# A two-layer hybrid trunk on one core: raw tokens into the first products, constants on another queue, a later rotation table and a shorter tail

## The chip, the cores and the metric

One core of one Trainium2 chip runs the whole program. The metric is the device time of one execution in microseconds (us). The engines are TensorE (PE in the profile; its weight loads are PEld), VectorE (DVE), ScalarE (ACT), GpSimd (POOL) and SyncE (SP). SP does no arithmetic: it issues DMAs, as ACT and POOL can too ("SPq", "ACTq", "POOLq").

## What is computed

The input x has 256 tokens of 1024 float32 values. Each of two layers normalises the stream, makes one large input projection, runs three token mixers side by side, projects and merges them, and adds the result to the stream:

```
for layer in range(2):
    h = rms_norm(x, norm_w[layer])                 # x * rsqrt(mean(x*x) + 1e-6) * norm_w
    proj = einsum('bsd,de->bse', h, w_in[layer])
    (a_xbc, a_z, a_dt, b_q, b_k, b_v, b_z,
     c_q, c_k, c_v, c_f, c_z, gates) = split(proj, split_at, axis=-1)
    y_a = mamba2_branch(a_xbc, a_z, a_dt, conv_w, conv_b, dt_bias, a_log, d_skip, ssm_norm_w)
    y_b = sliding_window_branch(b_q, b_k, b_v, b_z, sinks, cos, sin)
    y_c = forgetting_attention_branch(c_q, c_k, c_v, c_f, c_z, f_bias)
    branch = einsum('bsiw,iwd->bsid', stack([y_a, y_b, y_c]), w_proj[layer])
    merged = sum(sigmoid(gates + gate_bias) * branch)
    x = x + einsum('bsd,de->bse', merged, w_out[layer])
return rms_norm(x, final_norm_w)
```

The sliding-window branch rotates its queries and keys with a table of cosines and sines (`rope`). The document calls the projections by their letters: K, V and Q are `b_k`, `b_v`, `b_q`; CV is `c_v`; dt/f are the 16 columns of `a_dt` and the 16 of `c_f`.

## The kernel before

**Products.** Every product with a weight matrix is made in three passes of a reduced float32 format: each operand is split into a high part (`hi`, a copy on ACT, L259) and the rest (`lo`, a subtraction on DVE, L260; at the start half of them on POOL, L1149), and hi·hi, lo·hi and hi·lo are added up in one PSUM bank (`dense`, L273). Products of tokens in rows have the tokens' hi and lo as the stationary side; 256 tokens are two halves t of 128 rows. There are three PSUM banks for products (`mm`) and five for all else (`mx`).

**The stream of weights.** All weights come through one list, in the order in which the program uses them, as pieces of 512 KB. `load_to` (L327) issues them on SP's queue into six buffers named `raw`; `feed` (L358) splits a piece once fewer than four split pieces are held, and a new load is issued when a split has freed its buffer. The dt/f weights are a small load of their own in the same list (two DMAs, 64 KB), with their own split at L259 and L260. The hardware queues have eight lanes: a DMA waits for the landing of the one issued eight earlier.

**Order of the work.** PE's order is that of the program. Beside the list of products (from L1044) the program keeps a set of generators (attention, scan, transposes), which `launch` (L102) puts in with a due time, and `pump` and `drain` (L129, L139) take from between products by a clock of PE's work. The order on DVE, ACT and POOL is the scheduler's, except at the start, which is written out (L1136 on). In every engine the order, once built, is fixed: an instruction that waits holds all behind it.

**The start.** SP loads x's first 128 rows, the norm weight in all 128 partitions (`nwb`) and x's second rows, 512 KB each (L161 to L163), then the first six weight pieces. POOL's queue loads the rotation table (L190). PE makes 30 transposes of an identity (`WARM`). The squares' sums (L215, L1154) give the variance, `row_rstd` (L219 to L209) its inverse root; then h = x·rstd·nwb (L1160), transposes on PE (L100), hi and lo, and K's two products, with the transposes of the second rows in the first of them (`second_rows`). After K come V, then the layer's constants, then four Q products (heads 0 to 7 and 8 to 15, two halves of tokens), the small product for dt/f, and the gates of the window attention.

**Constants.** `layer_consts` (L403) issues nine small DMAs through `pdma`, which is ACT's queue in program order (L401): three into `vr`, four rows spread over 128 partitions into `hb`, and two loads of `d_skip` into `dsk`, each 64 partitions of eight single floats. For layer two it also loads `nwb`, and it is called towards the end of layer one.

**Rotation.** `rope` (L460) multiplies a product by the cosines (L465) and its swapped halves by the sines (L467, L468); POOL adds (L487 for K, L508 for Q).

**The convolution stage.** Eight "heavy" products with convolution (`u_conv`, L679) alternate with "light" ones: the two halves of CV (`u_cv`, L822) and gates.

**Merge and tail.** The branches' projections are merged (`merge`, L923) and transposed (`mT`, L938, with L934 and L935 as its split). `out_end` (L988) adds the output product to the residual (L991), takes the sum of squares on ACT (L215), multiplies by the final norm weight (L996), finds rstd (L1003, L226 on POOL, L228, L230) and scales 512 columns on DVE (L1006) and 512 on ACT (L1008).

Of the kernel before, what the change touches and what calls it, by code (L numbers as in the profile page):

```python
# [16 lines left out]
P = 128  # L17
S = 256
# [13 lines left out]
WARM = 30  # L32
# [11 lines left out]
def hybrid_trunk(  # L44
# [110 lines left out]

    tab = T("tab", [P, 1])
# [3 lines left out]
    nwb0 = T("nwb", [P, D])  # L160
    nc.sync.dma_start(x0[:, 0, :], x2[0:P, :])  # L161
    nc.sync.dma_start(nwb0, norm_w[0:1, :].to_broadcast([P, D]))
    nc.sync.dma_start(x0[:, 1, :], x2[P:S, :])  # L163
# [26 lines left out]
    nc.gpsimd.dma_start(rope_sb, rope_tab.rearrange("(t p) c d -> p t c d", p=P))  # L190
# [82 lines left out]
    def dense(pt, ah, al, bh, bl, w, after=None, mid=None):  # L273


        passes = ((ah, bh), (al, bh), (ah, bl))
# [4 lines left out]
        for i, (k, a, b) in enumerate(seq):  # L281
            mm(pt, a(k), b(k), start=(i == 0), stop=(i == len(seq) - 1))
            if after is not None:
                if i % 12 == 11:
                    after[i // 12]()
# [28 lines left out]
    raws, pieces, pieces_out = {}, {}, {}  # L314

# [11 lines left out]
    def load_to(j):  # L327

        while state["load"] < min(j, len(stream)):
# [3 lines left out]
            raw = T("raw" if n > 32 else "L1", [P, kper, n])  # L333
            for c, ap in src:
                m = ap.shape[-1]
                nc.sync.dma_start(raw[:, :, c:c + m],
                                  ap.rearrange("(k p) c -> p k c", p=P)[:, k:k + kper, :])
# [61 lines left out]
    y0.nwb = nwb0  # L399

    pdma = pin(nc.scalar.dma_start)  # L401
# [40 lines left out]
    def tok(ah, al, w, t, turn=True, mid=None, **kw):  # L442
# [3 lines left out]
        p = pmm()  # L446
# [13 lines left out]
    def rope(p, t):  # L460

        p4 = p.rearrange("p (h d) -> p h d", h=4)
        cos = bc(rope_sb[:, t, 0, :], 1, 4)
        a = T("L1", [P, 4, 64])
        tt(a, p4, cos, op=ALU.mult)  # L465
        b = T("L1", [P, 4, 64])
        tt(b[:, :, 0:32], p4[:, :, 32:64], bc(rope_sb[:, t, 1, 0:32], 1, 4), op=ALU.mult)  # L467
        tt(b[:, :, 32:64], p4[:, :, 0:32], bc(rope_sb[:, t, 1, 32:64], 1, 4), op=ALU.mult)  # L468
        return a, b

    def u_bkv(y, c0, t, after=None):

        def f(w):
            p = tok(y.hTh, y.hTl, w, t, turn=w.n == 512 or c0 > 0, after=after)
            if t == 0 and c0 == 0:
                kv = T("L8", [P, 2048])
                y.kT = kv[:, 0:1024].rearrange("p (h s) -> p h s", h=4)
                y.bv = kv[:, 1024:1536].rearrange("p (t c) -> p t c", t=2)
            if c0 > 0:
                act(halves(y.bv[:, t, :]), p, AF.Copy)  # L480
            elif w.n == 512:
                act(y.bv[:, t, :], p[:, 1, :], AF.Copy)
            if c0 == 0:
                a, b = rope(p if w.n == 256 else p[:, 0, :], t)
# [3 lines left out]
                launch(1, rest(kd), D_K)  # L488
# [10 lines left out]
    def u_bq(y, c0, t):  # L499

        def f(w):
            p = tok(y.hTh, y.hTl, w, t, turn=w.n == 512)
            for i in range(w.n // 256):
                if t == 0:
                    y.qT[c0 + i] = T("qt", [P, 2, S])
                a, b = rope(p if w.n == 256 else p[:, i, :], t)
                q = T("L1", [P, 4, 64])
                gtt(q, a, b, op=ALU.add)  # L508
                launch(1, rest(c0 + i, q.rearrange("p h d -> p (h d)")), D_Q)
# [90 lines left out]
    def swa_quad(y, c, qT):  # L600
        yield lambda: (1, 0) in y.zdone
# [220 lines left out]
    def u_cv(y, c, t):  # L822
        def f(w):
# [3 lines left out]
            act(halves(y.cv[:, t, c:c + w.n]), p, AF.Copy)  # L827
# [160 lines left out]
    def out_end(y, c, t, i, n, xo, p):  # L988
        sl = slice(c, c + n)
        with tc.high_priority():  # L990
            tt(halves(y.xn[:, t, sl]), p, halves(xo), op=ALU.add)  # L991
            sum_sq(y.xn, t, c, y.ss[t][:, i:i + 1], n)
            last = y.l + 1 == L
            nwb = fin["w"] if last else layers[y.l + 1].nwb
            if last:
                stt(y.xn[:, t, sl], y.xn[:, t, sl], -0.5, nwb[:, sl], op0=ALU.mult, op1=ALU.mult)  # L996
# [4 lines left out]
            if i == 2:  # L1001
                v = y.var[t][:, 1:2]
                stt(v, y.ss[t][:, 2:3], 1.0 / D, y.var[t][:, 0:1], op0=ALU.mult, op1=ALU.add)  # L1003
                r = row_rsqrt2(v)
                if last:
                    ts(y.xn[:, t, 0:512], y.xn[:, t, 0:512], r[:, 0:1], None, op0=ALU.mult)  # L1006
                    nc.sync.dma_start(out2[t * P:(t + 1) * P, 0:512], y.xn[:, t, 0:512])
                    act(y.xn[:, t, 512:D], y.xn[:, t, 512:D], AF.Copy, scale=r[:, 0:1])  # L1008
                    nc.scalar.dma_start(out2[t * P:(t + 1) * P, 512:D], y.xn[:, t, 512:D])
# [34 lines left out]
    for y in layers:  # L1044
        l = y.l
        w = w_in[l]
        y.gate, y.qT, y.ckT, y.sz, y.yh, y.yl, y.sq, y.h, y.ss, y.var, y.zdone, y.cqdone = {}, {}, {}, {}, {}, {}, [], {}, {}, {}, set(), {}
# [11 lines left out]
        def gates_proj(br):  # L1059
# [4 lines left out]
            def p(b):  # L1064
                c = 512 * b
                if b == 0 and br != 0:
# [11 lines left out]
        if l == 0:  # L1078
            k, v = cols(C_BK), cols(C_BV)
            op(k, u_bkv(y, 0, 0, [lambda j=j: second_rows(j) for j in range(2)]))  # L1080
            op(k, u_bkv(y, 0, 1))
# [19 lines left out]
        lights = [lambda: None, lambda: op(cols(C_CV, 512), u_cv(y, 0, 0), u_cv(y, 0, 1))]  # L1101
        lights += [lambda: None, lambda: op(cols(C_CV + 512, 512), u_cv(y, 512, 0), u_cv(y, 512, 1))]
        lights += [gp.pop(0), lambda: None, gp.pop(0), lambda: None]
        for (c0, u), light in zip(heavy, lights):
            op(cols(c0), u_conv(y, u, 0), u_conv(y, u + 1, P))
            light()
# [24 lines left out]


    ENG = mybir.EngineType
    with tc.manual_schedule(engines={ENG.PE, ENG.DVE, ENG.Activation, ENG.Pool}):
        load_to(N_RAW)
# [3 lines left out]
        ss = [T("ss", [P, 4], bufs=4) for _ in range(2)]  # L1139
        h = [T("L4", [P, D]) for _ in range(2)]  # L1140
# [76 lines left out]
```

## Time and profile before

| what | value |
|---|---|
| median of three runs | 847.56 us (847.43 to 850.89) |
| the profiled execution | 847.65 us |
| its span in the profile | 845.9 us |
| mean granted PE clock | 0.996 |
| PE, DVE, ACT, POOL busy | 833.4, 642.3, 511.6, 104.5 us |
| DMA traffic | 158.43 MB, mean 187 GB/s |

The span runs from the first to the last instruction that the profiler saw; the remaining 1.75 us lie around it. A row such as "L96 PE MATMUL mm<-hi,L" names the line of the kernel, the engine, the operation, the tile written and the tiles read; `L` stands for the tiles from shared pools (L1, L2, L4, L8). Brackets in the timeline give the engine's idle time before the row and what ended it.

### The profile page before, as it was taken

Reading aid. Unit: us, or ns where it says so; the run is one execution under the profiler, and the core shown is the slowest. Engines: PE = TensorE matmul, PEld = TensorE weight load, DVE = VectorE, ACT = ScalarE, POOL = GpSimd, SP = SyncE. Lnnn points to the kernel's source line nnn. Section 1 sums busy time; section 2 is a strip of 40 time slices with the busy share of each in tenths; the row PEclk is TensorE's granted clock in tenths of the full one; section 3 lists DMA queues with packets and bytes.
Section 4 is the critical chain, followed back from the end, with each engine's and each line's share of the span. In section 5 each row is a group of like instructions: output and inputs, shape, how many; then the busy total and the mean of one; then the engine's idle time right before and its main releaser. Section 6 shows DMA issues by size and latency. Waiting matters only on the chain.

```text
span 845.9 us, 15985 instructions
## 1 busy us (share of the span) xinstructions
PE 833.4 (99%) x5964; PEld 763.3 (90%) x5964; DVE 642.3 (76%) x1403; ACT 511.6 (60%) x1004; POOL 104.5 (12%) x134
## 2 busy tenths in 40 slices
PE   7999999999999999999999999999999999999996
PEld 7999898989999998888989998899899999988896
DVE  5777997998776679656788879879968667785665
ACT  6466777665666667435555667776557667654442
POOL 6310100000131010210014001000003110121000
PEclk9999999999999999999999999999999999999999
DMA  8666565666465545648676465465755555576632
GB/s 303 183 205 208 166 200 162 201 210 197 128 202 175 172 159 187 218 155 282 206 237 218 143 206 159 142 199 183 241 171 176 174 175 152 161 235 212 212 100 76
DMA packets 126638, 158.43 MB, mean 187 GB/s; under 512 B 12784, under 2 KB 88224, under 8 KB 126560
## 3 DMA queue, kind: packets, MB, share of 16 engines
q1 hardware_dynamic: 109456, 140.79, 52.9%
q10 hardware_dynamic: 17056, 16.49, 6.4%
q8 instruction: 47, 0.77, 0.4%
q14 instruction: 31, 0.25, 0.1%
q0 software_dynamic: 48, 0.13, 0.0%
HBM read 155.22 MB, written 2.16 MB: 186 GB/s over the span
## 4 chain that ended last, share of the span: by engine, by line
PE 95%; DMA 2%; ACT 0%; DVE 0%; issue 0%; POOL 0%; SPq 0%; POOLq 0%; DVEq 0%; ACTq 0%
PE mm L96 82%; PE mx L96 9%; PE mx L100 4%; DMA raw<-in_w_proj_dram 2%; DMA raw<-in_w_in_dram 1%; POOL lo L1149 0%; ACT hi L1148 0%; ACT hi L259 0%; ACT L L1008 0%; DVE L L260 0%; DVE L L935 0%; DVE L L934 0%; ACT L L259 0%; POOLq L1213 0%; ACT L L215 0%
## 5 line engine op out<-in xcount | busy, mean ns | idle before, releaser
L260 DVE TENSOR_TENSOR lo<-raw,hi 128x1024 fp32r<-128x1024 f32 x252 | 308.2, 1234 | 94.9 <-ACT hi L259 81.9
L96 PE MATMUL mm<-hi,L 128*128 128x512 f32 (+1 forms) x1344 | 373.9, 364 | 1.9 <-ACT hi L1148 1.4
L259 ACT ACTIVATE hi<-raw 128x1024 fp32r<-128x1024 f32 x252 | 263.2, 1056 | 93.0 <-PE mm L96 66.9
L96 PE MATMUL mm<-L,hi 128*128 128x256 f32 x1792 | 317.7, 278 | 0.0
L96 PEld LDWEIGHTS mm<-L,hi 128*128 128x128 f32 x1792 | 277.7, 192 | 6.8 <-issue 3.3
L96 PEld LDWEIGHTS mm<-hi,L 128*128 128x128 f32 x1344 | 241.5, 190 | 32.4 <-issue 2.7
L96 PE MATMUL mm<-L,lo 128*128 128x256 f32 x896 | 246.4, 275 | 0.0
L96 PE MATMUL mm<-lo,L 128*128 128x512 f32 (+1 forms) x672 | 241.3, 360 | 0.6 <-POOL lo L1149 0.6
L96 PEld LDWEIGHTS mm<-L,lo 128*128 128x128 f32 x896 | 171.9, 192 | 0.2
L96 PEld LDWEIGHTS mm<-lo,L 128*128 128x128 f32 x672 | 127.3, 190 | 15.4 <-POOL lo L1149 0.8
L862 POOL TENSOR_SCALAR_AFFINE_SELECT bias<-bias 128x128 f32<-128x128 f32 x64 | 35.7, 593 | 407.8 <-DMA bias<-cumd 232.7
L556 ACT ACTIVATE pp<-pp,nm 128x128 f32<-128x128 f32 (+1 forms) x128 | 56.5, 443 | 13.0 <-DVE nm L550 13.0
L693 DVE SCALAR_TENSOR_TENSOR L<-L,vec,L 128x255 f32<-128x255 f32 (+2 forms) x96 | 46.3, 482 | 4.8 <-ACT L L690 3.4
L96 PE MATMUL mx<-L,L 128*64 128x128 f32 (+1 forms) x384 | 34.4, 314 | 0.0
L886 ACT ACTIVATE L<-L 128x512 f32<-128x512 f32 x24 | 15.2, 632 | 30.2 <-DVE L L885 30.0
L568 DVE TENSOR_SCALAR pp<-pp,rsum 128x128 f32<-128x128 f32 (+1 forms) x128 | 32.1, 314 | 0.5
L696 ACT ACTIVATE L<-L 128x256 f32<-128x256 f32 x32 | 13.3, 417 | 31.4 <-DVE L L693 25.9
L96 PEld LDWEIGHTS mx<-L,L 128*64 128x64 f32 x384 | 22.9, 136 | 9.4 <-ACT pp L556 1.3
L777 ACT ACTIVATE L<-mm 128x256 f32<-128x256 f32 x48 | 18.1, 378 | 21.0 <-PE mm L96 21.0
L585 ACT ACTIVATE L<-mx 128x512 f32<-128x512 f32 x48 | 27.0, 596 | 2.7 <-PE mx L100 2.5
L100 PE MATMUL mx<-ident,pp 128*128 128x128 f32 x192 | 26.3, 273 | 0.0
L100 PE MATMUL mx<-ident,L 128*128 128x128 f32 x152 | 23.1, 279 | 1.6 <-DVE L L935 0.8
(173 smaller groups left out, 716.0 us busy)
## 6 DMA issues: line engine op xcount, KB each, us to landing
raw<-in_w_in_dram SPq DMA_DIRECT2D x200, 512.0 KB, 4.3
raw<-in_w_proj_dram SPq DMA_DIRECT2D x48, 512.0 KB, 5.6
raw<-in_w_out_dram SPq DMA_DIRECT2D x16, 512.0 KB, 5.1
L<-cumd ACTq DMA_DIRECT2D x8, 512.0 KB, 5.2
bias<-cumd ACTq DMA_DIRECT2D x16, 256.0 KB, 3.8
L<-in_gate_bias_dram ACTq DMA_DIRECT2D x12, 256.0 KB, 3.9
L<-in_x_dram SPq DMA_DIRECT2D x2, 512.0 KB, 5.0
nwb<-in_norm_w_dram SPq DMA_DIRECT2D x1, 512.0 KB, 5.4
```

Source lines behind the costliest of these rows:

```text
L96: nc.tensor.matmul(o, a, b, **kw)
L100: nc.tensor.transpose(o, a, i)
L259: keep(act)(hi, src, AF.Copy)
L260: keep(tt)(lo, src, hi.bitcast(F32), op=ALU.subtract)
L556: act(pp[:, i, sl], pp[:, i, sl], AF.Exp, scale=-1.0, bias=nm[:, e:e + 1], accum_out=sums[:, e:e + 1])
L568: ts(pp[:, i, sl], pp[:, i, sl], rs[:, 2 * i + b:2 * i + b + 1], 0.5, op0=ALU.mult, op1=ALU.mult)
L585: act(pT, pt, AF.Copy)
L693: stt(a[:, s:S], x_[:, 0:S - s], y.vec[:, 16 * j + u:16 * j + u + 1], a[:, s:S], op0=ALU.mult, op1=ALU.add)
L696: act(th, a, AF.Tanh)
L777: act(halves(th), p, AF.Tanh, scale=0.5)
L862: nc.gpsimd.affine_select(out=bias[:, i, dst], in_=bias[:, i, src], compare_op=ALU.is_ge, fill=NEG, base=0, pattern=[[-1, P]], channel_mul ...
L886: act(g, g, AF.Tanh, scale=0.5)
```

## The change

At the start, x's first rows come in two DMAs of 256 KB and the norm weight as eight rows of 128 on ACT's queue, turned by PE into one value for each partition (`nwT`). PE transposes raw x; DVE multiplies the transposes by `nwT` at the eviction (`xw`), and hi and lo are made of this. K, V, Q and the first half of CV of layer one are products of these tokens without rstd. Their evictions multiply by rstd, a value for each row (`y.rn`): in `rope` as a scalar beside the table, on ACT as a scale. K's evictions are put off until rstd is there (`late`), and K's first product lies in an `mx` bank.

While Q's and CV's products run, `normalize` multiplies the transposed tokens by rstd: ACT puts rstd on a diagonal, two products with ones spread it over the partitions, four multiplications on DVE and four splits give the tokens that everything after CV uses. CV's first half now stands directly behind Q, and the small dt/f load behind it in the stream.

`WARM` is 10 in place of 30, with ten further such transposes (`FILL`) behind the transposes of x's first rows. The first weight piece is loaded in two halves. The rotation table is loaded by SP behind x's second rows. `pdma` is SP's queue. The rotation adds of Q are in place, with longer delays for what follows in layer one. The window attention of layer one may start before its gates. The lights of the convolution stage are placed anew in both layers, and the split of the second branch in layer one comes earlier.

In the tail, the last sum of squares of the last layer is made by DVE, the variance stands ahead of the multiplication by the norm weight, and the final scale is 640 columns on DVE and 384 on ACT.

```diff
-WARM = 30
+WARM = 10
+FILL = 10
...
-    pdma = pin(nc.scalar.dma_start)
+    pdma = pin(nc.sync.dma_start)
...
-    def rope(p, t):
+    def rope(y, p, t):
...
+            if y.rn is None:
+                tt(o, i, bc(r, 1, 4), op=ALU.mult)
+            else:
+                stt(o, i, y.rn[:, t:t + 1], bc(r, 1, 4), op0=ALU.mult, op1=ALU.mult)
...
-                q = T("L1", [P, 4, 64])
-                gtt(q, a, b, op=ALU.add)
+                    gtt(a, a, b, op=ALU.add)
...
-            act(halves(y.cv[:, t, c:c + w.n]), p, AF.Copy)
+            act(halves(y.cv[:, t, c:c + w.n]), p, AF.Copy, scale=1.0 if y.rn is None else y.rn[:, t:t + 1])
...
             for c in (0, 2):
                 op(cols(C_BQ + 256 * c, 512), u_bq(y, c, 0), u_bq(y, c, 1))
+            op(None, lambda: launch(9, normalize(y0), 0.0))
+            op(cols(C_CV, 512), u_cv(y, 0, 0), u_cv(y, 0, 1))
+            op(None, lambda: normalized(y0))
...
+        if l == 0:
+            lights = {2: [lambda: cv(512)], 4: [gp.pop(0)], 6: [lambda: op(None, lambda y=y: split_late(y, 1))],
+                      7: [gp.pop(0)]}
+        else:
+            lights = {1: [lambda: cv(0)], 3: [lambda: cv(512)], 4: [gp.pop(0)], 6: [gp.pop(0)]}
...
+    def normalize(y):
+        rb = T("L1", [P, S])
+        for t in range(2):
+            act(rb[:, t * P:(t + 1) * P], ident, AF.Copy, scale=y.rn[:, t:t + 1])
+        yield 2.0
+        p = pmx()
+        for t in range(2):
+            mm(p[:, t * P:(t + 1) * P], ones, rb[:, t * P:(t + 1) * P], start=True, stop=True)
...
+                tt(xk, xk, bc(p[:, t * P:(t + 1) * P], 1, 4), op=ALU.mult)
+                split(hTh[:, t, k:k + 4, :], hTl[:, t, k:k + 4, :], xk)
...
+            if last and i == 2:
+                junk = T("L2", [P, 512])
+                nc.vector.tensor_tensor_reduce(out=junk[:, 0:n], in0=y.xn[:, t, sl], in1=y.xn[:, t, sl],
+                                               scale=1.0, scalar=0.0, op0=ALU.mult, op1=ALU.add,
+                                               accum_out=y.ss[t][:, i:i + 1])
...
+                    m = 640
```

The order of instructions changes at two places that matter below. First SP, from the weights of Q on. Before, the dt/f load (`L_72_373`) lies between two pieces of Q's weights:

```order
L336 DMA raw_311<-in_w_in_dram 128x2x512
L336 DMA raw_313<-in_w_in_dram 128x2x512
L336 DMA raw_315<-in_w_in_dram 128x2x512
L336 DMA raw_317<-in_w_in_dram 128x2x512
L336 DMA L_72_373<-in_w_in_dram 128x8x16 x2
L336 DMA raw_319<-in_w_in_dram 128x2x512
L336 DMA raw_325<-in_w_in_dram 128x2x512
L336 DMA raw_392<-in_w_in_dram 128x4x256
```

Now, at the same place, where `raw_290` is the last piece of Q, `raw_354` to `raw_449` are CV's first half and `L_91_461` is the dt/f load:

```order
L339 DMA raw_290<-in_w_in_dram 128x2x512
L339 DMA raw_354<-in_w_in_dram 128x2x512
L339 DMA raw_372<-in_w_in_dram 128x2x512
L254 DMA vr_375<-in_conv_w_dram 64x128
L254 DMA vr_375<-in_conv_b_dram 16x128
L254 DMA vr_375<-in_ssm_norm_w_dram 8x128
L254 DMA hb_379<-in_dt_bias_dram 128x16
L254 DMA hb_379<-in_f_bias_dram 128x16
L254 DMA hb_379<-in_sinks_dram 128x16
L254 DMA hb_379<-in_a_log_dram 128x16
L254 DMA dsk_384<-in_d_skip_dram 64x8x1 x2
L339 DMA raw_437<-in_w_in_dram 128x2x512
```

The constants, which stood in ACT's list between two evictions of K, stand between the second and the third piece of CV's weights. The dt/f load stands behind the fourth (`raw_449`).

Second DVE, around the split of the dt/f weights. Before (`L_123_587` is their split, `mm_413` the first Q product):

```order
L260 TENSOR_TENSOR lo_468<-raw_315,hi_467 128x1024
L260 TENSOR_TENSOR L_123_587<-L_72_373,L_123_587 128x8x32
L260 TENSOR_TENSOR lo_480<-raw_317,hi_479 128x1024
L465 TENSOR_TENSOR L_83_445<-mm_413,rope_98 128x256
L467 TENSOR_TENSOR L_84_447<-mm_413,rope_98 128x4x32
```

Now (`L_138_678` is their split, `mm_500` and `mm_547` are the last two Q products, `L_21_132` the transposed tokens that `normalize` multiplies):

```order
L260 TENSOR_TENSOR L_138_678<-L_91_461,L_138_678 128x8x32
L473 SCALAR_TENSOR_TENSOR L_105_534<-mm_500,rs_244,rope_98 128x256
L473 SCALAR_TENSOR_TENSOR L_106_535<-mm_500,rs_244,rope_98 128x4x32 x2
L473 SCALAR_TENSOR_TENSOR L_108_541<-mm_500,rs_244,rope_98 128x256
L473 SCALAR_TENSOR_TENSOR L_109_542<-mm_500,rs_244,rope_98 128x4x32 x2
L260 TENSOR_TENSOR lo_587<-raw_437,hi_586 128x1024
L260 TENSOR_TENSOR lo_599<-raw_449,hi_598 128x1024
L260 TENSOR_TENSOR lo_684<-raw_474,hi_683 128x1024
L473 SCALAR_TENSOR_TENSOR L_125_604<-mm_547,rs_244,rope_98 128x256
```

The split has moved from ahead of the first Q product's rotation to ahead of the third one's, and the lo parts of CV's last two pieces and the normalising stand behind it.

More of the change, by code (lines that the diff above doesn't have):

```diff
@@ L478, in f, with evict @@
                 y.bv = kv[:, 1024:1536].rearrange("p (t c) -> p t c", t=2)
+            (late.append if after is not None else lambda g: g())(lambda: evict(w, p))
+        def evict(w, p):
             if c0 > 0:
[L480 removed]
+                act(halves(y.bv[:, t, :]), p, AF.Copy, scale=y.rn[:, t:t + 1])
             elif w.n == 512:
```

203 lines of the change are left out of this document (128 added, 75 removed).

## The prediction

> **What bounds the kernel now.** First the page: how much of the span each engine works, and who is on the chain that ended last.
>
> ```profile
> span 845.9 us, 15985 instructions
> ...
> PE 833.4 (99%) x5964; PEld 763.3 (90%) x5964; DVE 642.3 (76%) x1403; ACT 511.6 (60%) x1004; POOL 104.5 (12%) x134
> ...
> PE 95%; DMA 2%; ACT 0%; DVE 0%; issue 0%; POOL 0%; SPq 0%; POOLq 0%; DVEq 0%; ACTq 0%
> ```
>
> PE is the bound. A change that hardly touches the matrix work can gain only where PE stands still or runs slowly: before the first product, at the half clock, in waits, and after the last product. Next, what PE waited for; the columns are us in total, times, longest.
>
> ```profile
> PE mm L96 <- ACT hi L1148: 1.4, 1, 1.4
> PE mx L100 <- DVE L L935: 0.8, 1, 0.8
> ```
>
> The first is at the very start. The second, in layer one's merge, is the one wait of any size between the start and the end. Then the table by stretches (PE busy, DVE, ACT, POOL, then granted clock, DMA share, GB/s):
>
> ```profile
> 12.00:14.00 2.00, 1.37 (x8) 1.17 (x7) 1.17 (x2) 1.26 (x3) 2.00 (x2) 0.75 1.09 355
> 14.00:16.00 2.00, 2.00 (x12) 2.00 (x11) 0.08 (x1) 1.32 (x3) 1.90 (x2) 0.50 1.06 390
> ```
>
> At 14 to 16 us the clock is 0.50, just where the first two products run. Up to about 17 us PE is starved or slow. So the profile leaves three places: some 17 us of start, the wait in the merge, and a tail of about 3.5 us after the last matmul.
>
> **The start: what is removed.** Rows of the timeline of before (start, duration, what; in brackets the idle time before):
>
> ```profile
> 4.47 0.63 ACT L215 ACTIVATE L<-L 128x512 f32<-128x512 f32 x1 [2.18 <-DMA L<-in_x_dram]
> ...
> 5.29 0.15 DVE L219 TENSOR_REDUCE sm<-ss 128x1 f32<-128x2 f32 x1
> ...
> 6.96 0.16 DVE L209 TENSOR_TENSOR rs<-sm,sm 128x1 f32<-128x1 f32 x1
> ...
> 8.03 0.63 ACT L215 ACTIVATE L<-L 128x512 f32<-128x512 f32 x1 [2.83 <-DMA L<-in_x_dram]
> ...
> 9.98 1.15 ACT L1148 ACTIVATE hi<-raw 128x512 fp32r<-128x512 f32 x2
> ...
> 10.66 1.50 PE L96 MATMUL mm<-hi,L 128*128 128x256 f32 x8 [1.38 <-ACT hi L1148]
> ```
>
> Before, the first 128 rows of x land at 4.4 us; squares and the rstd chain (5.29 to 7.12, 1.83 us) stand ahead of the transposes, and the first product begins at 10.66. In the changed kernel the transposes take raw x, so this chain leaves the path. I lay the new order out by these durations: x in two halves at 3.7 and 4.45; the first quarter megabyte of weights right behind, 5.2; ACT then works without a gap in pieces of 0.58 (9.98 and 1.15 for two), and its sixth piece, the last part that the first product needs, ends about 8.6. The first product ends about 10.95, the second, which needs the second rows' lo on DVE, 14.25. I take PE's clock as full here.
>
> By 14.25 before's kernel has not ended these two products: they run to 19.9 with V behind them. PE would be 5.6 us early. It cannot keep all of it, because K's rotation now needs rstd. The squares of the second rows are the last of ACT's list, 15.45; the chain's 1.83 makes 17.3; then two lo splits stand on DVE ahead of K's rotations.
>
> ```profile
> 826.61 2.35 DVE L260 TENSOR_TENSOR lo<-raw,hi 128x1024 fp32r<-128x1024 f32 x2
> ...
> 31.82 0.42 DVE L465 TENSOR_TENSOR L<-mm,rope 128x256 f32<-128x256 f32 x1 [1.71 <-PE mm L96]
> ...
> 32.55 0.41 DVE L465 TENSOR_TENSOR L<-mm,rope 128x256 f32<-128x256 f32 x1
> ```
>
> The pair takes 2.35 (19.6), each rotation 0.73 from one start to the next (21.1). The first Q product takes over the accumulator bank of the second K product, so it starts at 21.1, though V ends at 19.75: a new wait of 1.4. In before the same product starts here, after a 0.44 us piece of four transposes that the new order puts elsewhere:
>
> ```profile
> 25.91 0.68 PE L96 MATMUL mm<-hi,L 128*128 128x512 f32 x2
> ```
>
> 25.91 less 0.44 less 21.1: **4.4 us of gain, if nothing behind is late.**
>
> **The start: what is late next.** Two DMA matters. First, the layer's nine small constants leave ACT's queue, where they held ACT up for 5.24 us (the first row below), and stand on SP's, in the stream of weights, behind the fourteenth piece and ahead of the last two pieces of the new early product (CV). Second, the dt/f weights (64 KB) are now loaded behind these. Their split waits on ACT and DVE, which work in order; behind it on DVE stand two rotations, two lo splits of CV's weights, and the normalising of all tokens, on which everything after CV depends.
>
> ```profile
> 33.60 0.60 ACT L495 ACTIVATE L<-mx 128x512 f32<-128x512 f32 x1 [5.24 <-DMA hb<-in_dt_bias_dram]
> ```
>
> What the pair of d_skip loads (4-byte pieces) does to the weights is seen where layer two's constants are loaded, late in layer one: the issue, the queues from 366 to 376 us (packets, MB, share), and the stretches.
>
> ```profile
> 363.19 1.30 ACTq L254 DMA_DIRECT2D dsk<-in_d_skip_dram x2
> ```
>
> ```profile
> q10 hardware_dynamic: 1019, 0.01, 4.5%
> ```
>
> ```profile
> 374.00:376.00 2.00, 2.00 (x11) 1.76 (x10) 0.21 (x1) 0.00 (x0) 0.00 (x0) 1.00 0.03 0
> 376.00:378.00 2.00, 2.00 (x11) 1.73 (x10) 1.17 (x2) 0.00 (x0) 0.00 (x0) 1.00 0.79 294
> ```
>
> In ten us 1019 packets and 0.01 MB pass, and no weights: 0 GB/s up to 376, 12 us after the issue. In the new order the first of the pair waits for the fourteenth weight piece. That one is issued when DVE frees its buffer: 21.1 plus two splits beside POOL at 1.8 each, 24.7; and lands by the least time of these rows 3.9 later, 28.6.
>
> ```profile
> L260 DVE TENSOR_TENSOR lo<-raw,hi x2: 1762/1807/1852, 21.1 to 22.9; 128x1024 fp32r<-128x1024 f32 x2
> ...
> DMA to landing us min/median/max: 3.9/7.2/10.6
> ```
>
> So weights flow again at 40.4 (28.6 and 11.8); two pieces at some 350 GB/s (the stretches above show 355 and 390) are 3.0, and the small load, whose pair before took 3.8 from issue to landing, I put at 2.3 behind them: 45.7. Then in DVE's order: small split 46.5, two rotations 48.0, two lo splits 50.35, one more 51.5, two rotations 53.0, one lo 54.2, seven steps of the normalising at 0.62 to 58.5.
>
> ```profile
> L<-in_w_in_dram SPq DMA_DIRECT2D x2, 64.0 KB, 3.8
> ```
>
> ```profile
> 48.50 1.96 PE L96 MATMUL mm<-L,L 128*64 128x256 f32 x16
> ...
> 29.19 10.36 PE mm L96 x48
> ```
>
> The point to compare is the start of these 16 matmuls (dt/f). Before it is 48.50, without CV's first half; that half is 48 matmuls of 512 columns, 10.4 us by the second row (a Q pair). With 0.45 for four transposes moved ahead and 0.45 estimated for the two new ones-matmuls, the same work ends at 59.8. After: 58.5. **Gain left: 1.3 us.** PE alone would be there at 55.4. The bounds: if the pair blocks nothing, 4.4; if it blocks longer, each us costs one, past nothing.
>
> Other edits at the start: in-place rotation adds and longer delays only shift POOL work that has slack (12% busy); ten filler transposes stand where PE waits anyway; the rotation table, now behind x's second rows on SP, is 128 KB and needed only at 19.6, so nothing even if 3 us late; the deferred K evictions are in the sum.
>
> The filler is there for the clock. Transposes alone before the first product went like this in before:
>
> ```profile
> 5.00:6.00 1.00, 1.00 (x6) 1.00 (x6) 0.48 (x4) 0.20 (x2) 0.22 (x1) 1.00 0.92 307
> 6.00:7.00 1.00, 1.00 (x11) 1.00 (x9) 0.51 (x4) 0.00 (x0) 0.35 (x1) 1.00 1.00 398
> ```
>
> The same transposes go from 6 to 11 in a us at about 6.2: PE sped up with only transposes behind it. I take the row. The Trainium skill, page "TensorE: Matmul & The Clock Gate", section "Part 4: PE-mode transpose", says that the full clock does not engage for transposes, because they do not count as busy in the same way. By that rule the first products would start slow; the trace disagrees here, with 11 against 6.
>
> **The middle.** Layer one's light steps and the split for the second branch move by one or two heavies; PE's work is the same. CV leaves the heavies of the convolution stage, where DVE has no slack:
>
> ```profile
> 150.00:160.00 10.00, 10.00 (x83) 9.76 (x82) 10.00 (x20) 6.85 (x10) 0.00 (x0) 1.00 0.70 216
> ```
>
> PE is still full there, so I cost it at nothing, with up to 2 us if DVE falls behind.
>
> Layer two's constants, loaded late in layer one, stand on SP as well. ACT is freed, but the d_skip pair waits for the weight piece ahead of it and I put it 1 us later; what comes after it is the last branch's projection weights, on the chain:
>
> ```profile
> 369.82 12.77 DMA raw<-in_w_proj_dram
> ```
>
> The merge's wait of 0.8 follows from this, and would grow by as much. **Loss 1.0**; bounds 0.8 gained (the wait goes) to 2.0 lost.
>
> **The tail.** Rows after the last matmul, and one operation of the same size on DVE:
>
> ```profile
> 839.05 0.42 DVE L991 TENSOR_TENSOR L<-mm,L 128x256 f32<-128x256 f32 x1 [0.25 <-PE mm L96]
> 839.51 0.42 ACT L215 ACTIVATE L<-L 128x256 f32<-128x256 f32 x1 [1.69 <-DVE L L991]
> ...
> 840.39 0.15 DVE L1003 SCALAR_TENSOR_TENSOR sm<-ss,sm 128x1 f32<-128x1 f32 x1
> ...
> 841.73 0.72 ACT L1008 ACTIVATE L<-L,rs 128x512 f32<-128x512 f32 x1 [1.71 <-DVE rs L230]
> ```
>
> ```profile
> L550 DVE CUSTOM_DVE_ANT_0 pp<-mx,wmask,nsink 128x256 f32<-128x256 f32 x32 | 15.3, 477 | 0.0
> ```
>
> The squares now follow the add on DVE: 839.4 and 0.48 make 839.9, where v can start instead of at 840.39: 0.45 gained. The last scale on ACT is 384 columns for 512; between 0.42 for 256 and 0.63 for 512 (both in rows above) that is 0.1. **Gain 0.55**, bounds 0.3 and 0.7.
>
> **The sum.** The profiled execution took 847.65 us: the span and 1.75 around it, 0.1 above the median of 847.56. 847.65 less 1.3, less 0.55, plus 1.0 is **846.8 us**. A measurement of this kernel can tell about 0.5%, 4.2 us, from no change.
>
> **The rivals.**
>
> PE alone bounds the start: the d_skip pair costs the weights little, or the small load lands by 42.6, and the whole 4.4 stays. For it: in the first load the weights came back sooner, about 7 us after the first issue, since one piece stood between the two loads there:
>
> ```profile
> 36.00:38.00 2.00, 2.00 (x11) 1.76 (x10) 2.00 (x3) 1.99 (x3) 0.00 (x0) 1.00 0.04 0
> 38.00:40.00 2.00, 2.00 (x13) 1.76 (x12) 2.00 (x5) 0.20 (x1) 0.52 (x1) 1.00 0.14 27
> 40.00:42.00 2.00, 2.00 (x11) 1.73 (x11) 1.26 (x4) 0.47 (x2) 1.72 (x2) 1.00 0.69 212
> ```
>
> ```profile
> 32.22 1.34 ACTq L254 DMA_DIRECT2D dsk<-in_d_skip_dram x2
> ```
>
> Against: in the new order the pair stands together, as in the second load, where it was 12. 847.65 less 4.4, less 0.55 is 842.7, without the loss in the middle; 843.7 with it, 841.9 if the merge's wait goes. Chance 0.22, of which 0.19 below 843.4.
>
> Slower: on one queue the pair blocks the weights 18 us instead of 12, since each load then also holds the queue for the pieces issued behind it. The small load lands at 51.7, the 16 matmuls start 64.5, and the time is 847.65 plus 4.7, less 0.55, plus 1.0: 852.8. The whole is a loss when the small load lands past 46.6, and beyond 0.5% past about 50.7. Against: the row of 12. Chance 0.08.
>
> DVE bounds the convolution stage, where 10.00 of 10.00 leaves nothing: three heavies without a light between them make PE wait 2 us, 848.8. Chance 0.09.
>
> The first products run at half clock. In before, at the clock of 0.50:
>
> ```profile
> 14.33 2.06 PE L96 MATMUL mm<-hi,L 128*128 128x256 f32 x8
> ```
>
> At the full clock eight such would be 0.9 (10.36 for 48 of twice the columns). A loss of 1.2 on eight, some 1.5 before the clock comes up, passed on in full, is 848.3. Chance 0.03. This is where the skill's rule would lead.
>
> **How the numbers follow.** My forecast has the rest, 0.58, within 1.5 us either way by the spread of the landing times. The range 842.4 to 849.6 takes in the rivals but the slower one and the low corner of the first. Faster by over 0.5% (below 843.4): 0.19. Slower (above 851.8): 0.08. Within: 0.73.
>
> **What would show it.** Right: two K products done about 14 us; a PE wait of about 1.4 at Q0 on DVE; a hole in the DMA of some ten us from 29 to 40 without weights; ACT and DVE waiting for the small load at 45 us; the 16 matmuls at 58 to 59. Wrong: these matmuls at 55.5 with no wait ahead of them (first rival), past 62 (second), a DVE wait of PE between 150 and 200 (third), or a clock of 0.5 in the first products (fourth).

## The result, and the profile after

The changed kernel takes 856.24 us in the median (855.37 to 857.47), the kernel before 847.80 in the same runs: a ratio of 1.0094, interval 1.0077 to 1.0111. It is slower by 8.4 us, and outside the range that was given. The profile is of the slowest of the six, 857.47 us, and the sums below are for that one.

The page of the changed kernel, the same lines as of before:

```profile
span 855.8 us, 15968 instructions
...
PE 835.0 (98%) x5959; PEld 763.4 (89%) x5959; DVE 649.9 (76%) x1411; ACT 511.1 (60%) x1006; POOL 103.1 (12%) x129
...
PE 93%; DMA 3%; DVE 2%; SPq 1%; POOL 1%; issue 0%; ACT 0%; POOLq 0%; DVEq 0%; ACTq 0%
```

PE works as long as before (835.0 against 833.4), but it is on the chain for 93% where it was 95%: DMA, DVE, SP's queue and POOL have come onto it. PE's waits (us in total, times, longest) say where:

```profile
PE mx L101 <- POOL L L518: 8.3, 2, 4.6
PE mx L101 <- DVE L L945: 3.1, 1, 3.1
```

Two long waits at the start, for the rotation adds of Q on POOL (L518, formerly L508), and 3.1 in the merge in place of 0.8. The timeline shows the start (start, duration, what; in brackets the idle time before), of SP, ACT, POOL, DVE and PE:

```profile
29.99 1.32 SPq L254 DMA_DIRECT2D dsk<-in_d_skip_dram x2
...
32.55 11.07 SPq L339 DMA_DIRECT2D L<-in_w_in_dram x2
```

```profile
48.31 0.42 ACT L259 ACTIVATE L<-L 128x256 fp32r<-128x256 f32 x1 [12.30 <-DMA L<-in_w_in_dram]
```

```profile
50.17 0.73 POOL L518 TENSOR_TENSOR L<-L,L 128x256 f32<-128x256 f32 x1 [12.61 <-DVE L L473]
51.15 3.84 POOL L518 TENSOR_TENSOR L<-L,L 128x256 f32<-128x256 f32 x1 [0.24 <-DVE L L473]
```

```profile
49.10 1.91 DVE L473 SCALAR_TENSOR_TENSOR L<-mm,rs,rope 128x256 f32<-128x256 f32 x6
50.92 3.49 DVE L260 TENSOR_TENSOR lo<-raw,hi 128x1024 fp32r<-128x1024 f32 x3
```

```profile
50.96 0.44 PE L101 MATMUL mx<-ident,L 128*128 128x128 f32 x2 [4.62 <-POOL L L518]
55.04 0.69 PE L101 MATMUL mx<-ident,L 128*128 128x128 f32 x2 [3.65 <-POOL L L518]
...
65.69 1.96 PE L97 MATMUL mm<-L,L 128*64 128x256 f32 x16
```

Read from the top: the d_skip pair is issued at 29.99 (the first of the two waited from 28.96 for the landing of a weight piece, the DMA issued eight earlier); the two issues of the dt/f load behind it take 11.07; ACT waits 12.3 us for the dt/f load and splits it at 48.31; DVE splits behind it and makes the rotations of the third Q product; POOL adds; and PE, which has stood at the transposes of these rotated queries since 46.3, goes on. A second add takes 3.84 us in place of 0.73, all the time in which DVE runs three lo splits, and PE waits for that as well. The hole in the weights, and what the waits do to PE's clock (PE, PEld, DVE, ACT, POOL busy, then the granted clock, DMA share, GB/s):

```profile
38.00:40.00 2.00, 2.00 (x11) 1.76 (x10) 0.00 (x0) 0.00 (x0) 0.00 (x0) 1.00 0.03 0
...
46.00:48.00 2.00, 0.33 (x2) 0.00 (x0) 0.00 (x0) 0.00 (x0) 0.00 (x0) 1.00 0.21 21
48.00:50.00 2.00, 0.00 (x0) 0.00 (x0) 1.24 (x4) 1.69 (x3) 0.00 (x0) 1.00 0.94 285
50.00:52.00 2.00, 0.44 (x2) 0.20 (x2) 2.00 (x5) 2.00 (x4) 1.58 (x2) 0.92 1.07 354
52.00:54.00 2.00, 0.00 (x0) 0.00 (x0) 2.00 (x3) 1.88 (x5) 2.00 (x1) 0.50 1.09 366
54.00:56.00 2.00, 0.96 (x4) 0.87 (x5) 2.00 (x7) 0.36 (x2) 1.53 (x2) 0.50 1.09 350
56.00:58.00 2.00, 2.00 (x6) 1.63 (x5) 1.35 (x2) 0.15 (x1) 1.76 (x2) 0.50 1.09 347
58.00:60.00 2.00, 2.00 (x12) 1.69 (x10) 0.00 (x0) 0.20 (x1) 0.00 (x0) 0.87 1.07 345
```

PE stands from 46.3; some 5.4 us later the clock goes to 0.50 and stays there until 58.5, so PE's first matmuls behind the waits run at half speed. The same in the merge, smaller (the wait of before, then wait and clock of the changed kernel):

```profile
387.40 0.66 PE L100 MATMUL mx<-ident,L 128*128 128x128 f32 x4 [0.85 <-DVE L L935]
```

```profile
396.04 0.78 PE L101 MATMUL mx<-ident,L 128*128 128x128 f32 x4 [3.07 <-DVE L L945]
```

```profile
396.00:398.00 2.00, 1.96 (x8) 1.69 (x9) 1.69 (x3) 1.12 (x2) 0.00 (x0) 0.61 1.00 348
398.00:400.00 2.00, 2.00 (x7) 1.61 (x6) 0.18 (x1) 0.96 (x1) 0.00 (x0) 0.54 0.40 151
```

The last matmul of the changed kernel, from which its tail is counted:

```profile
848.76 0.28 PE L97 MATMUL mm<-lo,L 128*128 128x256 f32 x1
```

Where the time went, by marks that both programs have (us from the span's start):

| mark | before | after | later by |
|---|---|---|---|
| dt/f product starts (before: the 59.8 of the prediction, with the moved work) | 59.8 | 65.7 | 5.9 |
| the row of 96 matmuls behind the merge | 407.15 | 417.47 | 10.3 |
| last matmul | 838.74 | 848.76 | 10.0 |
| end of the span | 845.9 | 855.8 | 9.9 |

5.9 us are lost at the start and 4.4 more in the merge; 0.3 come back in layer two and 0.1 in the tail.

### The profile page after: what moved, and what is told of

The parts are those of the page before. It is cut to its first block, busy times and chain, and to the rows that moved or that the text cites. A ratio compares the mean times of both kernels' runs of the same rounds, so it can differ in the third digit from the quotient of the medians.

```text
span 855.8 us, 15968 instructions
## 1 busy us (share of the span) xinstructions
PE 835.0 (98%) x5959; PEld 763.4 (89%) x5959; DVE 649.9 (76%) x1411; ACT 511.1 (60%) x1006; POOL 103.1 (12%) x129
## 4 chain that ended last, share of the span: by engine, by line
PE 93%; DMA 3%; DVE 2%; SPq 1%; POOL 1%; issue 0%; ACT 0%; POOLq 0%; DVEq 0%; ACTq 0%
PE mm L97 79%; PE mx L97 9%; PE mx L101 5%; DMA raw<-in_w_proj_dram 2%; DMA L<-in_w_in_dram 1%; SPq L339 1%; POOL L L518 0%; DVE lo L260 0%; DVE L L473 0%; DVE lo L1225 0%; DVE L L1209 0%; DVE L L1217 0%; ACT hi L259 0%; ACT L L259 0%; DVE L L260 0%
## 5 line engine op out<-in xcount | busy, mean ns | idle before, releaser
L97 PEld LDWEIGHTS mm<-lo,L 128*128 128x128 f32 x664 | 126.0, 190 | 15.9 <-DVE lo L260 1.0
L872 POOL TENSOR_SCALAR_AFFINE_SELECT bias<-bias 128x128 f32<-128x128 f32 x64 | 32.7, 547 | 414.0 <-DMA bias<-cumd 247.8
L703 DVE SCALAR_TENSOR_TENSOR L<-L,vec,L 128x255 f32<-128x255 f32 (+2 forms) x96 | 46.3, 482 | 4.3 <-ACT L L700 3.1
L101 PE MATMUL mx<-ident,L 128*128 128x128 f32 (+1 forms) x153 | 24.0, 286 | 11.3 <-POOL L L518 8.3
L101 PEld LDWEIGHTS mx<-ident,L 128*128 128x128 f32 (+1 forms) x153 | 18.7, 146 | 15.0 <-POOL L L518 8.9
L260 DVE TENSOR_TENSOR L<-L,L 128x512 fp32r<-128x512 f32 (+1 forms) x38 | 20.6, 577 | 12.7 <-ACT L L259 12.6
```

The source lines that it names most:

```text
L97: nc.tensor.matmul(o, a, b, **kw)
L101: nc.tensor.transpose(o, a, i)
L260: keep(tt)(lo, src, hi.bitcast(F32), op=ALU.subtract)
L703: stt(a[:, s:S], x_[:, 0:S - s], y.vec[:, 16 * j + u:16 * j + u + 1], a[:, s:S], op0=ALU.mult, op1=ALU.add)
L872: nc.gpsimd.affine_select(out=bias[:, i, dst], in_=bias[:, i, src], compare_op=ALU.is_ge, fill=NEG, base=0, pattern=[[-1, P]], channel_mul ...
```

## The experiments

The chips' runs of the kernel before lay between 847.8 and 849.0, so runs are compared by their ratio to it; the changed kernel has 1.0094.

**What the constants cost, and why.** The first puts them back on ACT's queue:

```diff
-    pdma = pin(nc.sync.dma_start)
+    pdma = pin(nc.scalar.dma_start)
```

> The changed kernel with the layer constants back on ACT's queue; nothing else differs. Theory S (the stream): the loss comes from the two d_skip loads standing in SP's stream ahead of the dt/f load; without them there the dt/f split no longer holds ACT and DVE, the waits of 4.62 and 3.65 us before the transposes of Q go, and so does the half clock behind them: 10 us less at the start, and part of the merge's 4.4, so 842 to 847 us. Rival P (the place): the dt/f load behind CV's weights is late whatever queue the constants use; the time stays at 852 or more. Rival N (the new start): the raw-token start itself does not pay, because DVE and POOL get in each other's way; the time stays above the kernel before, 850 or more, with waits at Q's transposes. What speaks against S alone: on ACT's queue the constants hold ACT itself for some 5 us, as in before.

850.67 us, ratio 1.0030 (1.0013 to 1.0047). Above what theory S expected, below rival P's 852, and by its number just within rival N's 850 or more. The weights still stop, now from 32 to 38 us, the dt/f load is split at 43.87, and PE waits for what stands behind that split on ACT, an eviction of K:

```profile
32.00:34.00 2.00, 2.00 (x13) 1.81 (x12) 2.00 (x5) 0.00 (x0) 0.23 (x1) 1.00 0.05 0
...
36.00:38.00 2.00, 2.00 (x11) 1.76 (x10) 0.00 (x0) 0.00 (x0) 0.32 (x1) 1.00 0.04 0
```

```profile
43.87 0.42 ACT L259 ACTIVATE L<-L 128x256 fp32r<-128x256 f32 x1 [12.62 <-DMA L<-in_w_in_dram]
...
45.14 1.06 ACT L505 ACTIVATE L<-mx 128x512 f32<-128x512 f32 x2
```

```profile
PE mx L101 <- ACT L L505: 4.9, 1, 4.9
PE mx L101 <- DVE L L945: 2.4, 1, 2.4
```

So the queue alone is not the cause: the loads stop the weights from either, for some seven us from ACT's queue and some ten from SP's. The place on SP is worth 5.4 us of the loss by the ratios. The second experiment leaves them on SP and changes their form:

```diff
-            pdma(y.dsk[64 * half:64 * half + 64, :], src.to_broadcast([64, NK]))
+        pdma(y.drow.rearrange("p j two -> p (j two)"), d_skip[l:l + 1, :].to_broadcast([P, 2 * NK]))
...
+            pin(ts)(y.dsk[hs, :], y.drow[hs, :, half], 1.0, None, op0=ALU.mult)
```

> The changed kernel with the constants still on SP, but d_skip loaded as one row of 16 floats into all partitions (64-byte pieces, as the other rows) and laid out by two small DVE operations, in place of two loads of single floats. Theory S: the hole of 10 us without weights goes in both layers; start 10.3 us earlier, merge 4.4 or more: 841 to 844 us. Rival C (the queue): any nine small loads in SP's stream stop the weights; the hole stays and the time is 852 or more. Rival N: 850 or more, with waits at Q's transposes though the dt/f weights are there.

841.89 us, ratio 0.9917 (0.9886 to 0.9948): faster than before. PE's waits, its dt/f product, and the stretches that had no weights:

```profile
PE mx L97 <- POOL lo L1227: 0.6, 1, 0.6
PE mm L97 <- ACT L L1215: 0.5, 1, 0.5
PE mm L97 <- ACT L L259: 0.2, 1, 0.2
PE mm L97 <- DVE L L260: 0.2, 1, 0.2
```

```profile
55.76 1.96 PE L97 MATMUL mm<-L,L 128*64 128x256 f32 x16
```

```profile
30.00:32.00 2.00, 2.00 (x11) 1.71 (x10) 2.00 (x2) 1.52 (x3) 2.00 (x2) 1.00 0.13 15
32.00:34.00 2.00, 2.00 (x15) 1.87 (x14) 2.00 (x2) 1.95 (x3) 1.12 (x1) 1.00 0.19 19
34.00:36.00 2.00, 2.00 (x13) 1.76 (x12) 2.00 (x5) 0.18 (x1) 0.00 (x0) 1.00 0.87 313
```

Weights are back at 34 us, PE never waits over 0.6 us after its start, the merge's wait is gone. The loads of single floats are shown as the cause; the other small loads on SP leave a dip in the weights at 30 to 34 us, and PE has no wait from it. Rival C falls, and N with it.

**Place of the dt/f load.** In the stream ahead of CV:

```diff
+            dtf = sub([(0, w[:, C_DT:C_DT + 16]), (16, w[:, C_CF:C_CF + 16])], 32)
             op(cols(C_CV, 512), u_cv(y, 0, 0), u_cv(y, 0, 1))
```

> The changed kernel with the dt/f load ahead of CV's weights in the stream, and so ahead of the constants; these stay on SP with the single-float loads. Theory S: the weights still stop for 10 us, but no rotation stands behind a load that is late; CV's last two pieces land at about 43 to 45 us and hold PE a little instead, 1 to 4 us; the merge's excess of 4.4 stays: 847 to 851 us. Rival P: only the place of the dt/f load counts: the start is regained in full, 846. If the hole costs the same wherever the dt/f load stands (PE waits as long for CV's weights), 854 or more.

852.58 us, ratio 1.0052 (1.0031 to 1.0072), above theory S's 851 and below the 854 of the last case; rival P's 846 falls. The hole is the same; now ACT waits 14.07 us for a piece of CV's weights, and behind that wait stand the evictions of K: PE waits 6.0 for them.

```profile
45.66 1.06 ACT L259 ACTIVATE hi<-raw 128x1024 fp32r<-128x1024 f32 x1 [14.07 <-DMA raw<-in_w_in_dram]
```

```profile
PE mx L101 <- ACT L L505: 6.0, 1, 6.0
```

What waits first changes; that PE stands behind it does not. The place of the load alone is not the cause.

**The clock.** PE is kept busy through the two waits:

```diff
+            if y.l == 0 and t == 0 and c > 1:
+                fill = pmx()
+                for _ in range(42 if c == 2 else 33):
+                    nc.tensor.transpose(fill[:, 0:P], ident, ident)
```

> The changed kernel with 42 and 33 transposes of the identity put on PE ahead of the two transposes that wait (4.6 and 3.6 us at 0.109 us each); they fill the waits and add no other work. Theory S with the clock: 2.0 us of the loss at the start is PE at a clock of 0.50 after it stood still; with PE busy in the waits the clock stays at 1.00 and the time is 854.2 us, 2.0 less than the changed kernel. Rival, after the Trainium skill, page TensorE: Matmul & The Clock Gate, section Part 4: PE-mode transpose: transposes do not count as busy; then the clock falls all the same and the time is 856.2, or more by what the fillers overrun.

854.91 us, ratio 1.0065 (1.0038 to 1.0092); the dt/f product starts at 64.24, 1.45 us earlier.

```profile
50.00:52.00 2.00, 2.00 (x21) 2.00 (x19) 2.00 (x6) 2.00 (x4) 1.36 (x2) 1.00 1.09 370
52.00:54.00 2.00, 2.00 (x21) 2.00 (x20) 2.00 (x3) 1.76 (x4) 2.00 (x1) 1.00 1.09 353
54.00:56.00 2.00, 2.00 (x18) 1.78 (x17) 2.00 (x6) 0.73 (x3) 1.53 (x2) 1.00 1.09 348
```

The clock stays at 1.00 where it was 0.50. From the last of the waiting transposes to the dt/f product PE takes 8.97 us where it took 10.65, 1.7 less. That the half clock followed from PE standing still, and what it cost here, is shown by the profile; the times agree in direction, but their intervals overlap. The waits themselves remain.

**The two places apart.** The wide row for layer one alone:

```diff
+        if l == 0:
+            y.drow = T("drow", [P, NK, 2], bufs=2)
+            pdma(y.drow.rearrange("p j two -> p (j two)"), d_skip[l:l + 1, :].to_broadcast([P, 2 * NK]))
+        for half in range(2 * l):
```

> The changed kernel with d_skip as one row of 64-byte pieces for layer one alone; layer two's constants, loaded late in layer one, keep the two loads of single floats. Theory S, with the two places adding up: the start is regained, 9.9 us (65.69 to 55.76 at the dt/f product, as the wide row showed it), and the merge keeps its wait of 3.1 and its half clock behind it: 856.2 less 9.9 is 846.3 us, 845 to 848. If the wait in the merge came from the late start and not from the second pair of loads, it goes too: 842.

844.75 us, ratio 0.9947 (0.9927 to 0.9967), that is 14.7 thousandths under the changed kernel, or 12.5 us, where 9.9 were expected.

```profile
55.48 1.96 PE L97 MATMUL mm<-L,L 128*64 128x256 f32 x16
```

```profile
PE mx L101 <- DVE L L951: 1.7, 1, 1.7
```

The start is regained as expected (55.48). The merge's wait stays, so the second pair of loads makes it; but it is 1.7 and not 3.1, and the clock behind it does not fall. What sets its length is open. The place in the stream does not explain it: the pair is issued 15.8 us ahead of PE's transposes at 386.69 in the changed kernel, and 15.9 ahead of the same transposes here. In the six profiles with this pair on SP's queue the wait is 1.6 to 3.1, and the four executions of this kernel spread from 843.66, the profiled one, to 846.84. In the merge the clock held at waits up to 1.9 and fell at those of 2.4 (constants on ACT's queue) and more.

**The parts on the kernel before.** The wide row, and SP's queue, each alone:

```diff
-            pdma(y.dsk[64 * half:64 * half + 64, :], src.to_broadcast([64, NK]))
+        pdma(y.drow.rearrange("p j two -> p (j two)"), d_skip[l:l + 1, :].to_broadcast([P, 2 * NK]))
```

> The kernel before with d_skip as one row of 64-byte pieces in both layers, constants still on ACT's queue. It asks how much of the 841.9 us comes from the loads of single floats, that the kernel before has too. Theory S: they cost the kernel before little, since nothing late stands behind them: the wait of 0.8 in the merge goes, 846.5 to 847.5 us; the rest of the gain is the new start and the tail. Rival: the gain is the wide row's, whatever the start: 843 or less.

846.48 us, ratio 0.9963 (0.9951 to 0.9976): 3.1 us better by the ratio. The merge's wait is gone; the kernel's last matmul ends 1.6 us earlier than in the profile of before, of which 0.55 is there at the dt/f product already (47.95 for 48.50). More than expected, and still 0.0046 above the changed kernel with the wide row. The rival falls, but the single floats cost the kernel before something as well: 1.6 us by the profile, 3.1 by the times.

```diff
-    pdma = pin(nc.scalar.dma_start)
+    pdma = pin(nc.sync.dma_start)
```

> The kernel before with its constants on SP's queue, single floats and all; nothing else of the change. Theory S: at the start the loads stand behind the dt/f load and ahead of weights that PE needs only after 51 us, so nothing or up to 1 us there; in layer one's merge the wait grows as in the changed kernel, with the half clock behind it, some 4 us: 851 to 853 us. Rival: the merge's wait of the changed kernel comes from its new order of light steps: 847.8.

860.42 us, ratio 1.0130 (1.0113 to 1.0146), 11 us worse, and not where theory S had put it:

```profile
PE mx L100 <- POOL L L508: 7.1, 1, 7.1
PE mx L100 <- DVE L L935: 1.6, 1, 1.6
```

```profile
46.59 1.23 DVE L260 TENSOR_TENSOR lo<-raw,hi 128x1024 fp32r<-128x1024 f32 x1 [8.44 <-ACT hi L259]
```

Here too PE stands at the transposes of rotated queries, 7.1 us: this split of weights from behind the hole stands ahead of the rotations in DVE's list. In the profiled execution (857.02 us) the dt/f product is 8.6 later than in before, and the merge's wait grows by 0.8 without a fall of the clock. The wait grows with the old order of light steps too, so the rival falls. The move to SP with single floats alone costs the kernel before more than the whole change lost (0.0130 against 0.0094). Expectation and prediction made one error: both asked when PE itself needs the late data, and not what else is queued behind the wait for it.

**The filler.** The wide row, without the ten transposes ahead of the first product:

```diff
-FILL = 10
+FILL = 0
```

> The changed kernel with the wide row and without the ten filler transposes ahead of the first product (FILL is 0); PE then stands still from about 5.9 to 7.5 us. If the clock falls some 6 us after PE stood still, as it did behind the waits of the changed kernel, the first products run at 0.50 for a while near 12 to 16 us and the time is 1 to 2 us above the 841.9 of the same kernel with filler. If a gap of 1.7 us is too short for that, or transposes hold no clock: 841.9.

844.09 us, ratio 0.9935 (0.9921 to 0.9949) against 0.9917 with filler: the intervals overlap. The profile is clearer: the dt/f product starts at 56.75, 1.0 later.

```profile
8.00:10.00 2.00, 1.06 (x7) 0.86 (x6) 2.00 (x3) 1.52 (x3) 0.98 (x2) 0.72 1.06 365
10.00:12.00 2.00, 2.00 (x12) 2.00 (x11) 1.54 (x1) 0.25 (x2) 0.99 (x1) 0.50 1.10 363
```

The clock falls to 0.50 in the first products; with filler it stayed at 1.00. Ten transposes are worth about 1 us by the profile. PE's two waits ahead of the fall are only 1.04 and 0.94 us long: short waits close together were enough here, where one of 1.9 in the merge was not.

**The slow add.** The adds of Q in layer one on DVE:

```diff
-                    gtt(a, a, b, op=ALU.add)
+                    (tt if y.rn is not None else gtt)(a, a, b, op=ALU.add)
```

> The changed kernel with the rotation adds of Q in layer one made by DVE behind each pair of rotations, not by POOL. It asks what the second wait of 3.65 us is. Theory: it is POOL's second add, which took 3.84 us beside three lo splits of DVE where it takes 0.73 alone; on DVE two adds of 0.42 end some 0.8 us after the rotations, the first wait lasts about 5.1 in place of 4.6, the second is at most 0.4, and PE stands still a shorter time: 852.5 to 853.5 us in place of 856.2. Rival: the second wait is due to the late dt/f load like the first, and only changes its name: 856.

851.88 us, ratio 1.0052 (1.0031 to 1.0072), 0.0042 or 3.6 us under the changed kernel.

```profile
PE mx L101 <- DVE L L518: 5.1, 1, 5.1
```

One wait of 5.1 in place of two of 8.3 together, as expected: the second was POOL's add, and not the dt/f load. From PE's stop to the dt/f product it is 16.6 us in place of 19.4, so the slow add cost the start 2.8.

> The same adds on DVE, with the wide d_skip row. There POOL's slow add (3.85 us) hid behind PE's work, so by the theory nothing is gained, and DVE gets 8 adds of 0.42 more, 3.4 us, in the stretch ahead of the normalising: 841.9 us, or up to 1 us more if DVE becomes late. If the slow add still cost PE something there: 841 or less.

With the same edit and the wide row 841.54 us, ratio 0.9920 (0.9907 to 0.9933): as the wide row alone. Nothing waited for the slow add there.

**The tail and the queue, with the wide row.** In the first of these `out_end` is that of before; the second has this edit beside the wide row:

```diff
-    pdma = pin(nc.sync.dma_start)
+    pdma = pin(nc.scalar.dma_start)
```

> The changed kernel with the wide d_skip row and the tail of before (last sum of squares on ACT, scale 512 and 512). It prices the tail alone: by the prediction's term 0.55 us more than the 841.9 of the wide row, by the spans behind the last matmul (7.16 before, 6.81 to 7.04 in the changed ones) 0.1 to 0.35 more: 842.0 to 842.5.

842.28 us, 0.5 to 0.7 above the two kernels measured beside it that have the new tail (841.54 above and 841.81 below). Behind the last matmul the spans take 7.1 us with the old tail and 6.8 with the new: the tail is worth 0.3, the rest lies at the start.

> The changed kernel with the wide d_skip row and the constants back on ACT's queue. Theory S: without single floats the queue matters little; the nine issues take some 4 us of ACT's time near 22 us, which PE has no slack for only if ACT's splits of Q's weights come late: 842 to 844 us. If the move to SP is worth something by itself this is slower than the 841.9 by what it is worth; if not, equal within 0.5.

841.81 us, ratio 0.9922 (0.9909 to 0.9935): equal. Without single floats the queue of the constants does not matter, as theory S had it.

The fastest are three kernels that differ by less than their intervals: the changed one with the wide row, with either queue or with the adds on DVE (ratios 0.9917, 0.9922, 0.9920), 0.8% under the kernel before.

## Why the prediction was wrong, step by step

- **The bound: right. What PE alone would do: right in the number, in part by luck.** The prediction had PE at the dt/f product at 55.4 if nothing is late; with the wide row it was 55.76. On the way it had K's products done at 14.25 and a wait of 1.4 for K's rotations ahead of the first Q product, at 21.1. In the changed kernel K's products end at 15.77, and the first Q product starts at 20.96 with no wait, before the rotation of the second K product (21.85): it does not wait for that bank. The two errors cancel. (In before K's products end at 20.4 and not at 19.9; the sum does not use it.)
- **The hole: right in place and size.** Forecast: first d_skip load at 28.6, weights back at 40.4. Measured: 29.99, and weights from about 41. The two issues of the dt/f load then took 11.07 us on SP, and its split began at 48.31; the prediction had it land at 45.7. These 2.6 us are one part of the error.
- **What waits for the dt/f load: the step that failed.** The prediction added up DVE's list behind the split (to 58.5), put PE's own work beside it (to 55.4), and took the later one. But PE too has a fixed order, and in the middle of CV's first product stand the transposes of the third Q product, whose rotations are in DVE's list behind the split. PE stopped at 46.3 with 36 of the 48 matmuls of CV's first half still to do. The normalising, which the prediction took for the bound, was done at 65.1, before PE came to the dt/f product, and had itself waited 2.89 for PE. Not the later of two, but a sum: 55.4 and waits of 4.62 and 3.65 make 63.7; 65.69 was measured, and the 2.0 between are the slow clock (3.0 us at 0.50 and 2.0 at 0.87 account for 1.8). The slower rival asked for a late landing of this load, and its point, 46.6, was passed; its sign, these matmuls past 62, was there too. But its reason was not, since the weights stopped for some 11 us and not 18, and on its path a landing at 48.3 would have cost 1.7, not 8.
- **The adds on POOL at nothing: wrong**, by the 3.65 of the second wait (2.8 at the dt/f product, by the adds on DVE). The prediction argued with POOL's mean of 12%; what counted was DVE's list beside it.
- **The clock: wrong by omission.** The prediction asked only whether the first products would run at 0.50 (they did not, and the filler kept them from it), and not what a new wait does to the work behind it: 1.7 to 2.0 us at the start, and 1.7 in the merge (two us at 0.61 and two at 0.54).
- **The merge: right mechanism, wrong size.** Forecast 1.0, measured 4.4. The d_skip pair of layer two was issued at 370.88 where it was 363.19, 1.8 later than the 5.9 of the start explain; the products just ahead of the wait lost 0.5 to late splits (the wait begins at 392.97 where it began at 386.55, 6.4 later), the wait grew by 2.2, to 3.1, and the clock fell, 1.7 more. With a wait of 1.6 to 1.9, as in four other profiles, the forecast of 1.0 would have been near; why this one was longer stays open.
- **The convolution stage: right at nothing.** Up to the merge no further time was lost: the transposes ahead of its last products start at 380.77 in before and at 386.69 in the changed kernel, still 5.9 later.
- **The tail: mis-sized.** Forecast 0.55, with the lower bound 0.3; the spans show 0.1 and, with the wide row, 0.3.

By the measured terms: 847.65 and 5.9 and 4.4, less 0.3 and 0.1, make 857.6; the profiled execution took 857.47.

## What to carry to other kernels

When a load becomes late, follow it through every in-order list: the engine that splits it, what is queued behind that split, and which of this the matrix engine meets first in its own order, perhaps in the middle of unrelated work. Then it is a sum of waits and not the later of two ends. Look at the pieces of a small load and not at its bytes: 4 KB of single floats held up the weights for six to ten us, time for 2 to 3.5 MB at the 350 GB/s of other stretches; and price a wait of the matrix engine with the slow clock behind it, which cost some 1.7 us here, in the merge and at the start alike.

## What the hardware showed that was not expected

Two loads of 512 single floats each, 4 KB together, kept the weights from moving for about ten us from SP's queue (30 to 41 us in the changed kernel, with 0 GB/s at 38 to 40) and for six to ten from ACT's (in the kernel before 34 to 40 with at most 27 GB/s, and 366 to 376 for layer two; 32 to 38 with 0 GB/s in the changed kernel with the constants back there); the same 16 values in rows of 64 bytes to 128 partitions left a dip of some 4 us that the other constants share.

An add of POOL with two inputs in SBUF took 3.84 us where it takes 0.73, while DVE ran three lo splits with two such inputs at their usual 1.16 each. The Trainium skill, page "SBUF — State Buffer", section "SBUF: two separate sides", tells of a pair of ports that DVE and GpSimd share under an exclusive lock, so that the loser blocks fully instead of sharing; the trace agrees, with 3.26 us of the splits inside the 3.84. In the trace the add stays behind three instructions of DVE in a row, though the first of them alone had started before it.

By the granted clock of the stretches, PE's clock went to 0.50 at 51.7, 5.4 us after PE stopped, and came back at 58.5, 3.5 us after it worked again at 55.0; in the merge it was at 0.50 from 396.4 to 399.8. So the half clock lasted 6.8 us and 3.4 us; it lasted 3.4 us also in the kernel before (13.0 to 16.4) and without the filler (8.9 to 12.3). The Trainium skill, page "TensorE: Matmul & The Clock Gate", section "Part 1: The HAM clock gate (the "warmup" mystery)", gives free-running windows of about 3.4 us, one idle window to fall and one busy one to rise; the trace agrees on the length and not on idle: in the 3.4 us ahead of the fall PE had worked for 1.8 without the filler, and for 1.7 in the kernel before. The same page's rule on transposes, section "Part 4: PE-mode transpose", that the full clock does not engage for them, does not hold here: with transposes in the waits the clock stayed at 1.00, and without the ten ahead of the first product it fell.
